# Another order of the seven products of the down projection, T3 summed into B22 in place, and a fixed order for the last rows

## Chip, cores and metric

The kernel runs on one core of a Trainium2 chip. The metric is the device time of one execution in microseconds (us); all times below are in us unless marked ns. The engines are TensorE (PE in the profile; PEld is its weight load), VectorE (DVE), ScalarE (ACT), GpSimd (POOL) and SyncE (SP), which here only issues transfers.

## What is computed

One decoder layer on 512 rows of 1024 channels in float32: two attention mixers and their projections, then a gated MLP with a short convolution, then a last normalisation. Only the end is touched by the change:

```python
def _conv_ffn(h, w_up, conv_w, conv_b, w_down):
    ...
    return (jax.nn.gelu(a, approximate=False) * g) @ w_down
...
        x = x + gate2 * _conv_ffn(h2, w_up[l], conv_w[l], conv_b[l], w_down[l])
    return _rmsnorm(x, final_g)
```

The down projection multiplies 512 x 2816 activations by 2816 x 1024 weights. `_rmsnorm` divides each row by the root of its mean square and multiplies by the gain `final_g`.

## The kernel before

**Seven products.** The down projection (lines 1489 to 1697) is a Strassen-Winograd product. The inner dimension is split in 11 pairs (`NPR`) of two blocks of 128 (a = 0, 1), the activations in two halves of 256 rows, the weights in two halves of 512 columns. B11, B12, B21, B22 are the blocks `wblock(g, a, hf)`. Seven products replace eight. Each is a pass over six groups of pairs (`grp`: five of two pairs, the last of one); each pass has 11 x 2 x 3 = 66 matmuls of 512 columns, because every operand is split in a high and a low part and three products of parts are taken (`split`, lines 113 to 115: ScalarE casts the high part, VectorE subtracts it to get the low part).

The passes (lines 1537 to 1545) and the bank pair each writes:

- m1 into dX, with B11; then B12 is summed onto the weights;
- m5 into dZ, with B11 + B12; then B22 is summed on;
- m6 into dY, with B11 + B12 + B22; then B21 is summed on;
- m7 into dW, with T3 = B12 + B22;
- p3 with B22, added to m5 in dZ;
- p2 with B21, added to m1 in dX;
- p4 with the sum of all four blocks, added to m7 in dW.

**The sums of weights.** The first three and the last use `chain`, five and a half buffers of 512 KB that stay. Each sum is an accumulating transfer in GpSimd's queue (line 1655), issued once VectorE has read the old content. T3, B22 and B21 are `streamed` (lines 1510 to 1518): a plain load by SyncE into one of four rotating buffers (`raw_tile`), and for T3 a second, accumulating transfer in GpSimd's queue. Two of the T3 groups have buffers of their own (`spare`).

**The results.** After m1, m6, m7, p3 and p2 the function `after_pass` makes a list of VectorE steps (with squares on ScalarE), and the main loop (lines 1674 to 1697) puts them between the preparations of the next pass as `EACH` says. So `e2 -= dW` (line 1589) follows m7, `e -= dZ` (line 1599) follows p3, and dX is read (line 1611) after p2. `x1` holds the residual in four tiles of 128 rows, t = 0 to 3, and two halves, hf = 0, 1; `res(t, hf)` is such a piece. Row tiles 0 and 1 are finished after p2: `square` takes the sum of squares, `stat_start` and `stat_end` (with `rstd_start`, `rstd_end`, lines 167 to 184) the inverse root, whose power runs on GpSimd, and line 1622 scales by root and gain on VectorE. Row tiles 2 and 3 are finished by `last_tile`, one after the other.

**What sets the order.** Within this stage a scheduler orders the instructions of each engine as they are recorded; an engine then takes its queue strictly in order. Three buffers each hold the high and low weight parts (`WB = 3`), so a cast for group g waits until TensorE has used group g - 3. In the last pass groups 3 to 5 are held back (`HOLD = 3`) and multiplied first for tile 2, then for tile 3.

## Time and profile before

| | us |
|---|---|
| three runs | 722.17, 719.83, 722.52 (median 722.17) |
| the profiled execution | 720.56 |
| its span (first to last event on the core) | 718.7 |
| granted TensorE clock, mean of the span | 0.994 of full speed |
| down projection, first matmul | 601.79 after the span's start |
| last matmul | starts at 708.59 |

The prediction reads three kinds of lines. A row of the timeline has start, duration, engine, line, operation and operands, then how often it is repeated; brackets give idle time of the engine just before and what ended it. A row of busy time by stage has the stretch and its length, then busy time and number of instructions for PE, PEld, DVE, ACT and POOL, the granted clock, the share of the transfer engines and GB/s. A row of a group has line, engine, operation, operands, count, busy time, mean ns of one, and idle time before. Buffer numbers are left out of the names, so `dc` is any bank of dX, dZ, dY, dW, and `chain_kvA` to `chain_outl` are the four buffers of the chain. Names such as `p4wh`, `p4wl`, `p4a` are the high and low weight parts and the activations of pass p4.

### The profile page before, as it was taken

The page shows a single profiled execution, that of the slowest core. Times are in us where ns is not written, and L with a number is a line of the kernel's source. Part 1 is how long each engine was busy: PE and PEld are TensorE (multiplying, and loading weights), DVE is VectorE, ACT ScalarE, POOL GpSimd, SP SyncE. Part 2 cuts the span into 40 slices and gives each one's busy share as a digit, 9 for nine tenths or more (in the row PEclk, how much of TensorE's full clock was granted, in tenths as well). Part 3 has the DMA queues.
Part 4 walks back from the last instruction along what each step waited for, and adds up shares of the span by engine and source line. Part 5 has one row for each costly group of instructions (what it writes and reads, how often), then busy time and mean ns, then how long its engine had stood idle before and what let it go on. Part 6 is the DMA issues. An engine that isn't in the chain of part 4 may idle for free. (4 is left out here: it accounts for less than half of the span.)

```text
span 718.7 us, 11251 instructions
## 1 busy us (share of the span) xinstructions
PE 691.1 (96%) x4172; PEld 603.1 (84%) x4172; DVE 589.8 (82%) x1121; ACT 381.9 (53%) x672; POOL 84.9 (12%) x101
## 2 busy tenths in 40 slices
PE   6998899999999999999999999999999999999994
PEld 6776688777777888888888999999999999778883
DVE  6998877887986674865479899888888999889996
ACT  4643756355553333432358756555656666556662
POOL 4000000000100110000012111111101212640000
PEclk9999999999999999999999999999999999999998
DMA  9986122543543665736717698876879769998502
GB/s 313 305 242 205 60 60 67 169 136 106 169 139 126 206 190 162 235 101 210 246 59 148 162 190 204 207 183 200 201 197 223 161 175 256 206 207 221 178 0 118
DMA packets 117367, 124.70 MB, mean 174 GB/s; under 512 B 4511, under 2 KB 93376, under 8 KB 117312
## 3 DMA queue, kind: packets, MB, share of 16 engines
q1 hardware_dynamic: 98254, 97.71, 43.0%
q0 software_dynamic: 18720, 25.73, 21.0%
q8 instruction: 33, 0.54, 0.3%
q10 hardware_dynamic: 338, 0.54, 0.2%
q14 instruction: 22, 0.18, 0.1%
HBM read 121.85 MB, written 2.11 MB: 172 GB/s over the span
## 5 line engine op out<-in xcount | busy, mean ns | idle before, releaser
L1112 PE MATMUL up<-t,m_whi 128*128 128x256 f32 x528 | 96.1, 283 | 0.0
L1112 PEld LDWEIGHTS up<-t,m_whi 128*128 128x128 f32 x528 | 82.4, 192 | 0.0
L1112 PE MATMUL up<-t,m_wlo 128*128 128x256 f32 x264 | 74.7, 283 | 0.1
L1112 PE MATMUL up<-bh,p_wlo 128*128 128x256 f32 x232 | 65.6, 283 | 0.3 <-DVE p_wlo L1055 0.3
L1112 PE MATMUL up<-bh,p_whi 128*128 128x256 f32 x232 | 65.6, 283 | 0.0
L1112 PE MATMUL up<-bl,p_whi 128*128 128x256 f32 x232 | 65.6, 283 | 0.0
L1112 PEld LDWEIGHTS up<-t,m_wlo 128*128 128x128 f32 x264 | 50.6, 192 | 0.3 <-DVE m_wlo L1055 0.3
L748 DVE SCALAR_TENSOR_TENSOR arow<-ra,cs,arow 128x512 f32<-128x512 f32 x56 | 41.9, 748 | 4.3 <-DMA ra<-in_w_ada_dram 3.6
L1112 PEld LDWEIGHTS up<-bh,p_wlo 128*128 128x128 f32 x232 | 44.5, 192 | 0.5 <-DVE p_wlo L1055 0.5
L1112 PEld LDWEIGHTS up<-bh,p_whi 128*128 128x128 f32 x232 | 44.5, 192 | 0.0
L1112 PEld LDWEIGHTS up<-bl,p_whi 128*128 128x128 f32 x232 | 44.5, 192 | 0.0
L1023 POOL DMA_DIRECT2D s<-in_w_up_dram x21 | 27.3, 1379 | 142.5 <-DMA s<-in_w_up_dram 54.3
L1055 DVE TENSOR_TENSOR m_wlo<-s,m_whi 128x1024 fp32r<-128x1024 f32 x31 | 37.7, 1217 | 2.0 <-ACT m_whi L1051 2.0
L1051 ACT CAST m_whi<-s 128x1024 fp32r<-128x1024 f32 x31 | 32.5, 1047 | 8.5 <-PE up L1112 4.6
L174 POOL TENSOR_TENSOR r<-ms,mhalf 128x1 f32<-128x1 f32 (+1 forms) x16 | 13.6, 848 | 172.4 <-DVE ms L172 105.7
L1112 PE MATMUL up<-t,p_whi 128*128 128x256 f32 x176 | 32.2, 283 | 0.0
L678 ACT ACTIVATE sd<-sd,dmx 128x128 f32<-128x128 f32 (+3 forms) x32 | 17.8, 557 | 22.2 <-DVE dmx L676 15.7
L761 POOL DMA_DIRECT2D mod_rows<-arow x8 | 4.3, 541 | 203.5 <-ACT arow L760 203.4
L1112 PEld LDWEIGHTS up<-t,p_whi 128*128 128x128 f32 x176 | 27.5, 192 | 0.0
L1119 ACT ACTIVATE gT<-a,cv 128x512 f32<-128x512 f32 x22 | 17.7, 814 | 17.6 <-DVE a L1154 17.3
L1051 ACT CAST p_whi<-wa 128x1024 fp32r<-128x1024 f32 x18 | 18.8, 1043 | 12.0 <-PE up L1112 7.2
L1112 PE MATMUL up<-t,p_wlo 128*128 128x256 f32 x88 | 24.9, 283 | 0.0
(476 smaller groups left out, 2120.8 us busy)
## 6 DMA issues: line engine op xcount, KB each, us to landing
ra<-in_w_ada_dram SPq DMA_DIRECT2D x32, 512.0 KB, 4.2
wa<-in_w_up_dram SPq DMA_DIRECT2D x22, 512.0 KB, 4.2
s<-in_w_up_dram SPq DMA_DIRECT2D x21, 512.0 KB, 4.8
s<-in_w_up_dram POOLq DMA_DIRECT2D x21, 512.0 KB, 6.7
adaw<-in_w_ada_dram SPq DMA_DIRECT2D x16, 512.0 KB, 5.0
w<-in_w_in_dram SPq DMA_DIRECT2D x12, 512.0 KB, 4.8
a<-in_w_up_dram SPq DMA_DIRECT2D x11, 512.0 KB, 4.7
b<-in_w_down_dram SPq DMA_DIRECT2D x10, 512.0 KB, 3.6
```

Source lines behind the costliest of these rows:

```text
L174: nc.gpsimd.tensor_tensor(r0, ms, mhalf[:, :n], ALU.pow)
L678: nc.scalar.activation(pm[m], pm[m], AF.Exp, bias=mx[:, m : m + 1], scale=slope, accum_out=lsum[:, m : m + 1])
L748: nc.vector.scalar_tensor_tensor(ac, r[:, a], cc, ac, ALU.mult, ALU.add)
L761: nc.gpsimd.dma_start(mod_rows[idx : idx + 1, hf * S : (hf + 1) * S], row)
L1023: nc.gpsimd.dma_start(dst, upblock(*blk), accum_op=ALU.add)
L1051: nc.scalar.copy(W[J, name][0], R[J, SRC[name]])
L1055: nc.vector.tensor_sub(lo, R[J, SRC[name]], hi.bitcast(F32))
L1112: nc.tensor.matmul(o[u], w[:, k, cu], b[:, k], start=name in ("p1", "m5", "p2") and k == 0 and x == 0, stop=k == 3 and x == 2, skip_group_ ...
L1119: nc.scalar.activation(grow(j), av[J][:, u], AF.Identity, bias=cv[:, 66 + j : 67 + j], scale=cv[:, 44 + j : 45 + j])
```

## The change

The passes run in the order m1, m5, m6, p2, p3, m7, p4. T3 has no buffers and loads of its own: B22 is loaded once, and when p3 has split a group, B12 is summed onto it in place by GpSimd's queue, for m7. Two groups of B22 have buffers of their own. The lists of steps move with their passes (`e2 -= dW` is now among the steps of the last pass), and the list after p2 is spread thinner (`EACH`).

The gain is multiplied in on GpSimd for row tiles 0 and 1 (four pieces) and for the second half of row tiles 2 and 3. Row tiles 0 and 1 are finished after p3, and ScalarE scales them by the root, one copy of 128 x 1024 each.

The last rows are written out in a fixed order on VectorE, ScalarE, TensorE and GpSimd (`last_rows`): tile 2 whole, tile 3 in two halves of 256 columns, for which the held back matmuls of tile 3 are split in two.

```diff
-    spare = {4: big.tile([P, 2, S], F32, tag="hhB", name="t3_4"), 5: big.tile([P, 1, S], F32, tag="hlB", name="t3_5")}
+    second = {g: big.tile([P, 2, S], F32, tag=t, name=f"b22_{g}") for g, t in enumerate(("hhB", "hlB"))}
...
+    def streamed(g):
+        r = raw_tile([P, grp[g][1] - grp[g][0], S], f"b21_{g}")
+        nc.sync.dma_start(r, wblock(g, 1, 0))
+        return r
+
+    def seconds(g):
+        if g not in second:
+            second[g] = raw_tile([P, grp[g][1] - grp[g][0], S], f"b22_{g}")
+        nc.sync.dma_start(second[g], wblock(g, 1, 1))
+        return second[g]
+
+    def thirds(g):
+        return second[g]
...
-        ("m7", dW, streamed("t3", ((0, 1), (1, 1))), lambda g: ablock(g, 0, 1), None, None),
-        ("p3", dZ, streamed("b22", ((1, 1),)), lambda g: s4[:, slice(*grp[g])], None, None),
-        ("p2", dX, streamed("b21", ((1, 0),)), lambda g: ablock(g, 1, 0), None, None),
+        ("p2", dX, streamed, lambda g: ablock(g, 1, 0), None, None),
+        ("p3", dZ, seconds, lambda g: s4[:, slice(*grp[g])], (0, 1), None),
+        ("m7", dW, thirds, lambda g: ablock(g, 0, 1), None, None),
...
+                    nc.gpsimd.tensor_mul(e2[:, u], res(2 + u, 1), fgb[:, S:])
...
+                    stat_start(u)
+                    nc.gpsimd.tensor_mul(res(u, 1), res(u, 1), fgb[:, S:])
...
-                yield lambda u=u: V.tensor_mul(e2[:, u], res(2 + u, 1), fgb[:, S:])
+                def scale(u=u):
+                    nc.scalar.activation(x1[:, u], x1[:, u], AF.Copy, scale=stat_end(u))
+                    nc.sync.dma_start(od[u * P : (u + 1) * P, :], x1[:, u])
+                yield scale
...
-                    stat_start(u)
+                    nc.gpsimd.tensor_mul(res(u, 0), res(u, 0), fgb[:, :S])
...
-            for u in two:
-                def scale(u=u):
-                    rs = stat_end(u)
-                    for hf in two:
-                        V.scalar_tensor_tensor(
-                            res(u, hf), res(u, hf), rs, fgb[:, hf * S : (hf + 1) * S], ALU.mult, ALU.mult
-                        )
-                    nc.sync.dma_start(od[u * P : (u + 1) * P, :], x1[:, u])
-                yield scale
...
+    def last_rows(todo):
+        man = ExitStack()
+        man.enter_context(
+            tc.manual_schedule(engines={nc.vector.engine, nc.scalar.engine, nc.tensor.engine, nc.gpsimd.engine})
+        )
+        c0, c1 = slice(0, H), slice(H, S)
+        part = [partial(parts[2 + u, 1]) for u in range(2)]
+        for g in todo:
+            multiply(len(passes) - 1, g, 0)
+        for sl in (c0, c1):
+            for g in todo:
+                multiply(len(passes) - 1, g, 1, sl)
+        for t in tasks:
+            t()
+        last_mul(0)
+        s0 = last_add(0)
+        last_gain(0)
+        last_mul(1, c0)
+        r0 = rstd_start(s0, 1, D, bp, plus=part[0])
+        s1 = last_add(1, c0)
+        last_gain(1, c0)
+        rs0 = bp.tile([P, 1], F32, tag="rs2", bufs=4, name="rse0")
+        rstd_end(rs0, *r0, 1, bp)
+        partial(s1, part[1])
+        last_mul(1, c1)
+        s2 = last_add(1, c1)
+        r1 = rstd_start(s2, 1, D, bp, plus=s1)
+        last_gain(1, c1)
+        last_scale(0, rs0)
+        last_scale2(0, rs0, nc.sync)
+        rs1 = bp.tile([P, 1], F32, tag="rs2", bufs=4, name="rse1")
+        rstd_end(rs1, *r1, 1, bp)
+        last_scale(1, rs1)
+        last_scale2(1, rs1, nc.scalar)
+        man.close()
...
-            nc.gpsimd.dma_start(chain[g], wblock(g, *add), accum_op=ALU.add)
+            nc.gpsimd.dma_start(w, wblock(g, *add), accum_op=ALU.add)
...
-    EACH = {3: (0, 2, 2, 2, 1, 1), 4: (0, 0, 2, 2, 1, 1), 5: (0, 0, 2, 2, 2, 2), 6: (0, 0, 2, 2, 1, 1)}
+    EACH = {3: (0, 2, 2, 2, 1, 1), 4: (0, 0, 1, 1, 1, 1), 5: (0, 0, 2, 2, 2, 2), 6: (0, 0, 2, 2, 1, 1)}
```

`last_mul`, `last_add`, `last_gain`, `last_scale` and `last_scale2` are the steps of `last_tile`, each for one tile or one range of its columns: product with the gate out of the bank, sum with the residual and square, product with the gain, scaling of the first half on VectorE, scaling of the second on ScalarE.

More of the change, by code (lines that the diff above doesn't have):

```diff
@@ L1508, in ablock @@
         return gT4[g][:, :, a, hf * H : (hf + 1) * H]
-    def streamed(name, blocks):
-        def get(g):
-            n = grp[g][1] - grp[g][0]
-            r = spare[g] if name == "t3" and g in spare else raw_tile([P, n, S], f"{name}_{g}")
-            nc.sync.dma_start(r, wblock(g, *blocks[0]))
-            for b in blocks[1:]:
-                nc.gpsimd.dma_start(r, wblock(g, *b), accum_op=ALU.add)
-            return r
-        return get
+    def streamed(g):
[9 more added lines that the diff above has]
+        return second[g]
     for g in range(len(grp)):
@@ L1628, in last_tile, with last_mul @@
-    def last_tile(u):
-        t = 2 + u
-        v = m1[:, u]
-        nc.vector.tensor_mul(v, dW[u], gate(0))
-        nc.vector.tensor_add(res(t, 0), res(t, 0), v)
-        square(t, 0)
-        nc.vector.tensor_mul(v, res(t, 0), fgb[:, :S])
-        stat_start(t)
-        rs = stat_end(t)
-        nc.vector.tensor_scalar_mul(res(t, 0), v, rs)
-        (nc.sync, nc.scalar)[u].dma_start(od[t * P : (t + 1) * P, :S], res(t, 0))
-        nc.scalar.activation(res(t, 1), e2[:, u], AF.Copy, scale=rs)
-        (nc.scalar, nc.sync)[u].dma_start(od[t * P : (t + 1) * P, S:], res(t, 1))
+    def last_mul(u, sl=slice(0, S)):
+        nc.vector.tensor_mul(m1[:, u, sl], dW[u][:, sl], gate(0)[:, sl])
@@ new lines, in last_add, with last_gain @@
+    def last_add(u, sl=slice(0, S)):
+        nc.vector.tensor_add(res(2 + u, 0)[:, sl], res(2 + u, 0)[:, sl], m1[:, u, sl])
+        sq = big.tile([P, S], F32, tag="sq2", name=f"sqe{u}_{sl.start}")
+        s1 = bp.tile([P, 1], F32, tag="ss2", bufs=8, name=f"sse{u}_{sl.start}")
+        nc.scalar.activation(sq[:, sl], res(2 + u, 0)[:, sl], AF.Square, accum_out=s1)
+        return s1
+    def last_gain(u, sl=slice(0, S)):
+        nc.vector.tensor_mul(m1[:, u, sl], res(2 + u, 0)[:, sl], fgb[:, sl])
@@ new lines, in partial, with last_scale, last_scale2 @@
+    def partial(s1, plus=EPS):
+        nc.vector.tensor_scalar(s1, s1, 1.0 / D, plus, ALU.mult, ALU.add)
+        return s1
+    def last_scale(u, rs):
+        nc.vector.tensor_scalar_mul(res(2 + u, 0), m1[:, u], rs)
+        nc.sync.dma_start(od[(2 + u) * P : (3 + u) * P, :S], res(2 + u, 0))
+    def last_scale2(u, rs, q):
+        nc.scalar.activation(res(2 + u, 1), e2[:, u], AF.Copy, scale=rs)
+        q.dma_start(od[(2 + u) * P : (3 + u) * P, S:], res(2 + u, 1))
+    def last_rows(todo):
[33 more added lines that the diff above has]
+        man.close()
@@ L1658, in prepare, with multiply @@
         ops[i, g] = ah, al, wh, wl
-    def multiply(i, g, u):
+    def multiply(i, g, u, sl=slice(0, S)):
         name, bank2 = passes[i][:2]
@@ L1669, in multiply @@
                 nc.tensor.matmul(
-                    bank2[u], a[:, q, cu], b[:, q], start=first_mm and x == 0, stop=last_mm and x == 2,
+                    bank2[u][:, sl], a[:, q, cu], b[:, q, sl], start=first_mm and x == 0, stop=last_mm and x == 2,
                     skip_group_check=name not in first,
@@ L1682 @@
                 next(tasks)()
-        assert next(tasks, None) is None
         tail = HOLD if i == len(passes) - 1 else 0
@@ L1688 @@
         if tail:
-            for u in range(2):
-                for g in range(NG - tail, NG):
-                    multiply(i, g, u)
-                last_tile(u)
+            last_rows(range(NG - tail, NG))
         else:
```

## The prediction

> **What bounds the kernel now.** I read the page's busy shares first, then busy time by stage, then TensorE's rows for its gaps, then the rows of the other queues around each gap.

> ```profile
> span 718.7 us, 11251 instructions
> PE 691.1 (96%) x4172; PEld 603.1 (84%) x4172; DVE 589.8 (82%) x1121; ACT 381.9 (53%) x672; POOL 84.9 (12%) x101
> ...
> 480.00:520.00 40.00, 40.00 (x336) 40.00 (x335) 34.74 (x50) 22.98 (x35) 4.83 (x6) 1.00 0.81 201
> 601.60:633.60 32.00, 30.84 (x136) 24.82 (x135) 28.79 (x43) 19.00 (x27) 16.33 (x14) 1.00 1.06 207
> 633.60:693.50 59.90, 59.66 (x263) 49.42 (x264) 54.47 (x75) 37.10 (x56) 6.92 (x6) 1.00 0.65 165
> 693.50:709.00 15.50, 15.47 (x68) 12.17 (x66) 14.66 (x29) 7.07 (x13) 1.51 (x3) 1.00 0.17 69
> 709.00:718.70 9.70, 0.00 (x0) 0.00 (x0) 4.03 (x11) 2.17 (x4) 1.06 (x2) 0.76 0.28 108
> ```

> TensorE (first pair of each stage row) is busy nearly everywhere, and only the down projection (601.6 onwards) is touched. Its seven passes of 66 matmuls run at full clock; VectorE (third pair) has 54.5 us of work in 59.9, so it is never far ahead. A change gains where TensorE waits now or after its last matmul, and loses where it makes TensorE wait. These are the rows where it waits, starts the last pass, and ends:

> ```profile
> 622.90 0.50 PE L1669 MATMUL dc<-m5wl,m5a 128*128 128x512 f32 x1 [0.27 <-DVE m5wl L115]
> ...
> 632.33 0.39 PE L1669 MATMUL dc<-m6wh,m6a 128*128 128x512 f32 x1
> 633.84 0.50 PE L1669 MATMUL dc<-m6wl,m6a 128*128 128x512 f32 x1 [1.13 <-DVE m6wl L115]
> ...
> 693.59 0.39 PE L1669 MATMUL dc<-p4wh,p4a 128*128 128x512 f32 x1
> ...
> 704.82 0.50 PE L1669 MATMUL dc<-p4wl,p4a 128*128 128x512 f32 x1
> ...
> 708.59 0.39 PE L1669 MATMUL dc<-p4wh,p4a 128*128 128x512 f32 x1
> 710.39 0.68 DVE L1631 TENSOR_TENSOR pairs<-dc,g2b 128x512 f32<-128x512 f32 x1
> 714.12 0.72 ACT L1639 ACTIVATE x<-chain_outl,rsd 128x512 f32<-128x512 f32 x1 [1.56 <-DVE rsd L184]
> 714.87 0.33 SPq L1640 DMA_DIRECT2D out_dram<-x  x1
> ```

> From 633.84 to 693.59 are 263 matmuls, 0.227 each, so a pass is 15.0. The last matmul ends at 708.98 (708.59 + 0.39), the last arithmetic at 714.84, 5.86 later; the last store fills the rest of the span.

> **The change, part by part.** I keep the clock of before: p2 and m7 trade the fourth and sixth of seven slots, p3 stays fifth, p4 last.

> *T1, sums taken out of the crowded start.* GpSimd's queue sums T3 early now; the change sums b12 into b22 during p3.

> ```profile
> 610.86 1.20 POOL L1516 DMA_DIRECT2D t<-in_w_down_dram  x1 [5.44 <-DMA t<-in_w_down_dram]
> 611.68 1.62 POOL L1655 DMA_DIRECT2D chain_kvB<-in_w_down_dram  x1
> ...
> 620.54 1.05 ACT L114 CAST m5wh<-chain_kvB 128x1024 fp32r<-128x1024 f32 x1 [2.88 <-DMA chain_kvB<-in_w_down_dram]
> ...
> 621.62 1.23 DVE L115 TENSOR_TENSOR m5wl<-chain_kvB,m5wh 128x1024 fp32r<-128x1024 f32 x1 [3.06 <-ACT m5wh L114]
> ```

> One T3 sum holds the queue for 5.44 until its first half has landed. Behind it stand the chain sums; kvB's arrives so late that ScalarE idles 2.88 and VectorE 3.06, and VectorE, hardly idle from there to m6, delivers m5wl and m6wl late. Without that wait kvB is issued some 4 earlier, and one 512 KB sum fewer runs beside it. Both stalls should go. Price: 632.33 to 633.84 is 1.51 where 0.23 is normal (1.28); the m5 gap is 0.27 plus the 0.16 by which a 0.39 matmul normally overlaps its successor; each restart takes 0.50 rather than 0.39 (0.22 for both). Sum -1.9, from 0 (all stays) to -1.9.

> *T2, p4 behind m7 in the same banks.* This decides. Now p4 adds to dW long after L1589 has read m7's result from it. Afterwards p4 follows m7 directly, so its first matmul must wait until that subtraction (`e2 -= dW`) has read the bank. In the built program's order VectorE reaches that subtraction only after the low halves of p4's groups 0, 1 and 2.

> ```profile
> 663.18 0.69 DVE L1589 TENSOR_TENSOR chain_outl<-chain_outl,dc 128x512 f32<-128x512 f32 x1 [0.44 <-PE dc L1669]
> ...
> 688.44 1.29 DVE L115 TENSOR_TENSOR p4a<-gT,p4a 128x512 fp32r<-128x512 f32 x2
> 688.61 0.19 ACT L1552 ACTIVATION_READ_ACCUMULATOR sqd<-x 128x1 f32 x1
> 689.70 1.06 ACT L114 CAST p4wh<-chain_kvA 128x1024 fp32r<-128x1024 f32 x1 [0.91 <-PE dc L1669]
> ...
> 690.79 1.23 DVE L115 TENSOR_TENSOR p4wl<-chain_kvA,p4wh 128x1024 fp32r<-128x1024 f32 x1 [1.06 <-ACT p4wh L114]
> ...
> 693.90 1.05 ACT L114 CAST p4wh<-chain_kvB 128x1024 fp32r<-128x1024 f32 x1
> ...
> 695.45 1.22 DVE L115 TENSOR_TENSOR p4wl<-chain_kvB,p4wh 128x1024 fp32r<-128x1024 f32 x1
> ```

> Floor: the cast for group 2 takes the buffer of the previous pass's last group, so it cannot start before that pass's last matmul ends, at 693.75 (one 0.227 before 693.59, plus 0.39; the row has 693.90). Cast 1.05, low half 1.22, subtraction 0.69, handoffs 0.1: p4 starts at 696.8 at best, +3.2. Had the subtraction stood first (as L1589 did at 663.18) it would cost some 0.3.

> ScalarE makes it later. Row tiles 0 and 1 are now scaled by ScalarE (two 128x1024 copies), and in its queue both stand ahead of p4's first cast. The second copy needs the inverse root of row tile 1, which needs GpSimd's power, which stands in GpSimd's queue behind a product by the gain of the same tile, which needs the second square (accumulator read until 688.80). With d for one GpSimd product: 688.80 + 0.1 + d, power 0.6, two small VectorE steps 0.45, copy 1.0 gives p4's first cast at 690.95 + d. From there to the end of the subtraction: cast and handoff 1.1, three low halves 1.14 apart, one p4a 0.6 (two took 1.29), subtraction and handoff 0.74, in all 5.85.

> ```profile
> L150 POOL TENSOR_SCALAR_AFFINE_SELECT ddf<-ddf 128x512 f32<-128x512 f32 x1 | 0.6, 608 | 0.0
> L435 POOL MEMSET va<- 128x2048 f32 x1 | 1.8, 1804 | 0.0
> ...
> 367.90 0.68 DVE L1253 TENSOR_TENSOR early<-wa,early 128x512 fp32r<-128x512 f32 x1
> 368.07 0.93 POOL L174 TENSOR_TENSOR r<-ms,mhalf 128x1 f32<-128x1 f32 x1 [3.68 <-DVE ms L172]
> ...
> 373.37 0.69 DVE L1232 TENSOR_TENSOR bl<-braw,bh 128x512 fp32r<-128x512 f32 x1
> 373.53 0.93 POOL L174 TENSOR_TENSOR r<-ms,mhalf 128x1 f32<-128x1 f32 x1 [4.53 <-DVE ms L172]
> 377.01 0.55 POOL L174 TENSOR_TENSOR r<-ms,mhalf 128x1 f32<-128x1 f32 x1 [2.54 <-DVE ms L172]
> ```

> No GpSimd product of 128x512 is in the trace. One of one input took 0.61; I take d = 1.2 for two inputs, with ends 0.6 and 1.8 (the longest GpSimd arithmetic row). That gives a first cast at 692.15 and p4 at 698.0, +4.4 (+3.8 to +5.0).

> The last rows say more. The power took 0.93 twice when a VectorE sum or difference of two SBUF tiles was running, and both times it ended 0.4 after that one (368.58, 374.06); without one it took 0.55. So GpSimd waited. Whether a long GpSimd product holds VectorE likewise no row shows; I take it that it does, since the exclusion is there in one direction. VectorE here runs little but such differences. Then the two products of the slot cost VectorE, ahead of the second root, about 1.2 each, less what its gaps hide: +2.2, from +1.4 (GpSimd gets in behind the running difference) to +3.2 (it waits for a gap). T2 = +6.6; bounds +3.2 and +8.2. [...]

> *T3, VectorE relieved.* These instructions leave VectorE:

> ```profile
> L1622 DVE SCALAR_TENSOR_TENSOR x<-x,rsd,fgbr 128x512 f32<-128x512 f32 x4 | 2.8, 746 | 0.0
> L1608 DVE TENSOR_TENSOR chain_outl<-x,fgbr 128x512 f32<-128x512 f32 x2 | 1.3, 688 | 0.0
> ```

> That is 4 x 0.746 + 2 x 0.688 = 4.4. But TensorE felt VectorE's load after m6 only at 704.82, a restart of 0.50 that lost some 0.2: -0.2. Elsewhere the matmuls themselves hid these instructions, so the rest of the relief is worth nothing.

> *T4, the last tile in two column halves.* 336 matmuls of mostly 256 columns took 40.00, 0.119 each; 30 of them against 15 of 0.227 is +0.2.

> *T5, after the last matmul.* Now VectorE reaches the last tile 1.41 after 708.98, held by the tile before. Afterwards that tile's three steps run under the last 3.6 of matmuls. But the first half's VectorE product has, in the built program, its wait on the very last matmul, so the halves don't overlap: one half's three steps come ahead of the other's chain. A half step I estimate at 0.4, between half of 0.68 and all of it. The chain of a whole tile is 4.45 now (710.39 to 714.84); three half steps ahead add 1.2, the shorter product, sum and square take 0.8 off, the other tile's small statistics in between add 0.35: 5.2 against 5.86, -0.6 (0 to -1.4). The stores are as now.

> Sum: -1.9 + 6.6 - 0.2 + 0.2 - 0.6 = +4.1.

> The profiled execution took 720.56 (1.9 outside its span); the median shown is 722.17 (719.83 to 722.52). The mean of the four is 721.3, and on it I put the sum: 725.4.

> **The rivals.**

> *No mutual hold.* GpSimd products run beside VectorE: T2 = +4.4 and the sum is +1.9, 723.2, not measurably slower. For it: no row shows VectorE held. Against: the two rows of 0.93. The point is whether the second root is ready by about 691.

> *The in-place sum comes late.*

> ```profile
> 660.92 1.22 DVE L115 TENSOR_TENSOR p3wl<-b,p3wh 128x1024 fp32r<-128x1024 f32 x1
> ...
> 674.74 1.06 ACT L114 CAST p2wh<-b 128x1024 fp32r<-128x1024 f32 x1 [0.91 <-PE dc L1669]
> ...
> chain_kvA<-in_w_down_dram POOLq DMA_DIRECT2D x6, 512.0 KB, 10.2
> t<-in_w_down_dram POOLq DMA_DIRECT2D x5, 512.0 KB, 7.1
> ```

> b12 may be added only when p3's split has read b22 (slot five, 662.14), and m7's cast wants it 12.6 later. Sums took 7 to 10 in the crowded stretch; here they run almost alone. From 12.6 on each microsecond goes to the split. At 13, with the last two sums also behind a GpSimd product, I estimate +2: 727.4.

> *Not slower.* VectorE takes the subtraction from dW as soon as m7 ends, as L1589 did at 663.18: T2 is +0.3 instead of +6.6, and with T5 at its end the sum is -1.9 + 0.3 - 0.2 + 0.2 - 1.4 = -3.0, 718.3. It decides if the bank is free before p4's first low half is needed. The order of the built program speaks against it; it is also the price if my reading of that wait is wrong.

> **How the numbers follow.** Forecast 0.58, no hold 0.28, late sum 0.10, not slower 0.04. The forecast's own range is 723.5 to 728 (T2 from +5.8 to +8.2, T1 from -1.9 to -1). About 0.5% (3.6) is what a measurement of this kernel can tell from no change; the forecast lies on both sides of that: 0.42 of its 0.58 above, the late sum all above, no hold all within, the last rival half within and half beyond on the fast side. So faster 0.02, same 0.46, slower 0.52. The range 722.0 to 728.8 reaches from no hold with T5 near its end to the late sum with a T2 of 8, and leaves out the last rival and the far ends.

> **What would show it.** T1: no gap at m5 and m6, kvB's sum near 607. T2: one TensorE gap of 3 to 8 ahead of p4's first matmul, ended by the subtraction from dW, with ScalarE's two row copies ahead of p4's first cast. The hold: GpSimd products of 128x512 and VectorE rows that start when these end; without it the gap is near 4.4. T5: 5.2 from the last matmul to the last copy. The prediction is wrong if there is no gap before p4, or if gaps appear inside m7 (late sums).

## The result and the profile after

Medians of four runs each: 728.50 (727.06 to 729.48) after, 721.32 (719.83 to 722.52) before. The ratio is 1.0094, 95% interval 1.0077 to 1.0111: about 6.8 us slower. The forecast was 725.4. The profiled execution took 728.95, its span is 727.2.

The first row is the page's busy shares of the changed kernel; compare PE with 691.1 before:

```profile
PE 693.7 (95%) x4187; PEld 605.9 (83%) x4187; DVE 590.6 (81%) x1119; ACT 383.1 (53%) x676; POOL 95.0 (13%) x107
```

TensorE is busy 2.6 us longer for the same work, so part of that work ran slower. Busy time by stage, the six passes up to m7, then the gap in two pieces, then p4 in two pieces (the granted clock is the number after the last "x" group):

```profile
603.40:693.20 89.80, 89.80 (x398) 74.10 (x396) 82.86 (x117) 54.14 (x80) 35.74 (x29) 1.00 0.85 166
693.20:697.50 4.30, 0.17 (x1) 0.00 (x0) 2.06 (x4) 4.00 (x6) 0.00 (x0) 1.00 0.59 244
697.50:700.60 3.10, 0.00 (x0) 0.00 (x0) 3.10 (x5) 1.74 (x3) 0.00 (x0) 0.50 0.00 0
700.60:704.30 3.70, 3.64 (x9) 2.90 (x10) 3.70 (x7) 0.09 (x1) 0.10 (x1) 0.50 0.00 0
704.30:717.80 13.50, 13.50 (x74) 11.57 (x72) 6.60 (x10) 5.01 (x10) 2.83 (x2) 1.00 0.01 2
```

The first six passes run without a break. Then TensorE stands still, and from 697.5 to 704.3 its clock is at half. TensorE's own rows at the places shown before, and around p4's start:

```profile
603.40 0.40 PE L1719 MATMUL dc<-m1wh,m1a 128*128 128x512 f32 x1
...
633.37 0.39 PE L1719 MATMUL dc<-m6wh,m6a 128*128 128x512 f32 x1
633.60 0.39 PE L1719 MATMUL dc<-m6wl,m6a 128*128 128x512 f32 x1
...
692.99 0.39 PE L1719 MATMUL dc<-m7wh,m7a 128*128 128x512 f32 x1
700.66 0.77 PE L1719 MATMUL dc<-p4wh,p4a 128*128 128x512 f32 x1 [7.28 <-DVE chain_outl L1594]
701.22 0.63 PE L1719 MATMUL dc<-p4wl,p4a 128*128 128x512 f32 x1
701.65 1.05 PE L1719 MATMUL dc<-p4wh,p4a 128*128 128x512 f32 x2
...
717.52 0.28 PE L1719 MATMUL dc<-p4wh,p4a 128*128 128x256 f32 x1
```

At m6 the second matmul follows after 0.23, where 1.51 passed before. p4 would have started at 693.22 and starts at 700.66: **a gap of 7.44**, ended by the subtraction from dW. The next matmuls start 0.43 apart instead of 0.227. The p4 pass takes 17.14 (700.66 to 717.80), before 15.39. The three other queues ahead of p4, each from the timeline. GpSimd's, from kvB's first sum on:

```profile
609.48 1.20 POOL L1705 DMA_DIRECT2D chain_kvB<-in_w_down_dram  x1 [2.44 <-DVE m1wl L115]
...
686.69 1.46 POOL L1613 TENSOR_TENSOR x<-x,fgbr 128x512 f32<-128x512 f32 x1 [10.15 <-ACT sqd L1557]
688.31 1.82 POOL L174 TENSOR_TENSOR r<-ms,mhalf 128x1 f32<-128x1 f32 x1 [0.16 <-DVE ms L172]
690.10 1.28 POOL L1613 TENSOR_TENSOR x<-x,fgbr 128x512 f32<-128x512 f32 x1
692.23 0.93 POOL L174 TENSOR_TENSOR r<-ms,mhalf 128x1 f32<-128x1 f32 x1 [0.84 <-DVE rsd L184]
```

VectorE's, with the first step after the last matmul as its last row:

```profile
686.90 1.26 DVE L172 SCALAR_TENSOR_TENSOR ms<-ssd,ssd 128x1 f32<-128x1 f32 x1
...
690.16 1.25 DVE L180 SCALAR_TENSOR_TENSOR rt<-r,ms 128x1 f32<-128x1 f32 x1 [0.46 <-POOL r L174]
691.33 0.68 DVE L115 TENSOR_TENSOR p4a<-gT,p4a 128x512 fp32r<-128x512 f32 x1
691.93 0.15 DVE L172 SCALAR_TENSOR_TENSOR ms<-ssd,ssd 128x1 f32<-128x1 f32 x1
...
693.45 0.16 DVE L184 SCALAR_TENSOR_TENSOR rsd<-rt,r 128x1 f32<-128x1 f32 x1
695.82 2.36 DVE L115 TENSOR_TENSOR p4wl<-chain_kvA,p4wh 128x1024 fp32r<-128x1024 f32 x2 [2.21 <-ACT p4wh L114]
698.09 0.69 DVE L115 TENSOR_TENSOR p4a<-gT,p4a 128x512 fp32r<-128x512 f32 x1
698.70 1.22 DVE L115 TENSOR_TENSOR p4wl<-chain_kvB,p4wh 128x1024 fp32r<-128x1024 f32 x1
699.83 1.28 DVE L1594 TENSOR_TENSOR chain_outl<-chain_outl,dc 128x512 f32<-128x512 f32 x2
...
717.84 0.42 DVE L1632 TENSOR_TENSOR pairs<-dc,g2b 128x256 f32<-128x256 f32 x1 [1.45 <-PE dc L1719]
```

ScalarE's, with the last arithmetic as its last row:

```profile
692.25 1.15 ACT L1617 ACTIVATE x<-x,rsd 128x1024 f32<-128x1024 f32 x1 [2.66 <-DVE rsd L184]
693.70 1.15 ACT L1617 ACTIVATE x<-x,rsd 128x1024 f32<-128x1024 f32 x1 [0.30 <-DVE rsd L184]
694.75 1.98 ACT L114 CAST p4wh<-chain_kvA 128x1024 fp32r<-128x1024 f32 x2
...
722.59 0.72 ACT L1653 ACTIVATE x<-chain_outl,rse 128x512 f32<-128x512 f32 x1 [0.89 <-DVE rse L184]
```

Read them as one chain: GpSimd's first product (686.69), VectorE's step `ms` beside it (686.90), the first power (688.31), VectorE's first root step (690.16), a split of p4's activations (691.33), the second `ms` (691.93), the second power (692.23), the second root (693.45), ScalarE's second copy (693.70), p4's first casts (694.75), three low halves, the subtraction (699.83), TensorE. The second product (690.10) is on the chain because the root step of 690.16 waits beside it: VectorE steps on a 128x1 column take 1.26 and 1.25, each ending when a GpSimd product ends; without one the same steps take 0.15 and 0.22. From the first matmul of m1 to the end of the last arithmetic (the **stage**) it is 119.91, before 113.05: +6.86, the whole loss.

The stage starts 1.6 later in this profile (603.40 against 601.79), for a reason far ahead of it, in code that the change leaves alone. Busy time of one stretch there:

```profile
60.00:80.00 20.00, 16.89 (x85) 12.33 (x86) 15.05 (x50) 8.63 (x27) 0.00 (x0) 0.83 0.50 161
```

It is the stretch from 60 to 80 of the changed kernel, at a granted clock of 0.83; in the kernel before it is 1.00. Over the profiles of this study the stage starts between 599.9 and 603.4. So kernels are compared below by the stage where a term is wanted, and by the ratio, against the kernel before on the same chip, for the whole.

### The profile page after: what moved, and what is told of

It reads as the page before. It is cut to its first block, busy times and chain, and to the rows that moved or that the text cites. A ratio compares the mean times of both kernels' runs of the same rounds, so it can differ in the third digit from the quotient of the medians.

```text
span 727.2 us, 11282 instructions
## 1 busy us (share of the span) xinstructions
PE 693.7 (95%) x4187; PEld 605.9 (83%) x4187; DVE 590.6 (81%) x1119; ACT 383.1 (53%) x676; POOL 95.0 (13%) x107
## 2 busy tenths in 40 slices
DMA packets 115864, 121.83 MB, mean 168 GB/s; under 512 B 4415, under 2 KB 93280, under 8 KB 115808
## 5 line engine op out<-in xcount | busy, mean ns | idle before, releaser
L174 POOL TENSOR_TENSOR r<-ms,mhalf 128x1 f32<-128x1 f32 (+1 forms) x16 | 14.5, 904 | 120.0 <-DVE ms L170 54.7
L678 ACT ACTIVATE sd<-sd,dmx 128x128 f32<-128x128 f32 (+3 forms) x32 | 17.8, 557 | 22.2 <-DVE dmx L676 15.4
## 6 DMA issues: line engine op xcount, KB each, us to landing
ra<-in_w_ada_dram SPq DMA_DIRECT2D x32, 512.0 KB, 4.2
wa<-in_w_up_dram SPq DMA_DIRECT2D x22, 512.0 KB, 4.1
s<-in_w_up_dram SPq DMA_DIRECT2D x21, 512.0 KB, 4.9
s<-in_w_up_dram POOLq DMA_DIRECT2D x21, 512.0 KB, 6.4
adaw<-in_w_ada_dram SPq DMA_DIRECT2D x16, 512.0 KB, 4.8
w<-in_w_in_dram SPq DMA_DIRECT2D x12, 512.0 KB, 4.4
a<-in_w_up_dram SPq DMA_DIRECT2D x11, 512.0 KB, 4.6
b<-in_w_down_dram SPq DMA_DIRECT2D x10, 512.0 KB, 4.0
```

The lines of the kernel that those rows point to most:

```text
L174: nc.gpsimd.tensor_tensor(r0, ms, mhalf[:, :n], ALU.pow)
L678: nc.scalar.activation(pm[m], pm[m], AF.Exp, bias=mx[:, m : m + 1], scale=slope, accum_out=lsum[:, m : m + 1])
```

## Experiments

All start from the changed kernel unless said. "Pass" is p4's, from its first matmul to the end of the last, "tail" from there to the end of the last arithmetic.

| kernel | ratio (95%) | gap | pass | tail | stage |
|---|---|---|---|---|---|
| before | 1 | 0 | 15.39 | 5.86 | 113.05 |
| after | 1.0094 (1.0077 to 1.0111) | 7.44 | 17.14 | 5.51 | 119.91 |
| e1 gains on VectorE | 0.9971 (0.9958 to 0.9983) | 0.35 | 15.43 | 5.46 | 111.03 |
| e2 subtraction earlier | 1.0047 (1.0034 to 1.0060) | 5.69 | 17.43 | 5.52 | 118.44 |
| e3 copies later | 1.0006 (0.9994 to 1.0018) | 2.34 | 17.02 | 5.52 | 114.67 |
| e4 roots and copies behind p4 | 0.9960 (0.9948 to 0.9972) | 0.35 | 15.98 | 5.63 | 111.79 |
| e5 TensorE busy, 100 matmuls | 1.0132 (1.0102 to 1.0161) | filled | 15.41 | 5.51 | 121.83 |
| e6 early sums again | 1.0033 (1.0012 to 1.0053) | 0.35 | 15.96 | 5.64 | 117.40 |
| e7 e1 + GpSimd products | 1.0021 (1.0005 to 1.0038) | 2.72 | 15.43 | 5.46 | 114.51 |
| e8 e1 + GpSimd memsets | 0.9963 (0.9935 to 0.9990) | 0.35 | 15.44 | 5.46 | 111.04 |
| e9 e1, last tile whole | 0.9952 (0.9935 to 0.9969) | 0.35 | 15.24 | 4.86 | 110.25 |
| e10 TensorE busy, 64 matmuls | 1.0061 (1.0040 to 1.0081) | filled | 15.42 | 5.52 | 118.16 |
| e12 memsets for products | 1.0055 (1.0034 to 1.0076) | 4.97 | 18.00 | 5.52 | 118.30 |

Gap, pass, tail and stage are those of one profiled execution; the ratio is over all runs. In e2 and e6 the two differ by some 2 us (stage +5.4 and +4.4 against before, ratio worth +3.4 and +2.4; e6's twelve runs lie between 718.06 and 728.40). Why isn't shown.

**The chain ahead of p4 (e1 to e4).**

```diff
-                    nc.gpsimd.tensor_mul(res(u, 1), res(u, 1), fgb[:, S:])
+                    nc.vector.tensor_mul(res(u, 1), res(u, 1), fgb[:, S:])
```

(e1; so for all three such lines.)

> The changed kernel with its six 128x512 products by the gain on VectorE instead of GpSimd; all else as changed (in the built order VectorE then also takes the subtraction from dW one low half earlier). Theory A (the wait ahead of p4 is made by the chain GpSimd product, power, second root, ScalarE's row copies, p4's casts): the power comes early, the gap ahead of p4 falls from 7.4 to 0.3-0.6, TensorE's clock stays at 1.00 after it, the p4 pass takes 15.4-15.6 instead of 17.1, and the time is about 719.5 (728.5 - 7.1 - 1.75). Theory B (the floor of the prediction: p4's third cast must wait for m7's last matmul and the subtraction stands behind it): gap 3.2 or more, 723 to 724.

TensorE's row of e1:

```profile
693.57 0.47 PE L1719 MATMUL dc<-p4wh,p4a 128*128 128x512 f32 x1 [0.19 <-DVE chain_outl L1594]
```

The wait for the subtraction is still there and costs 0.35. 719.27, faster than before: theory A. In its built order VectorE takes the subtraction behind p4's first low half, so theory B's floor no longer applies; e1 alone doesn't tell how much is GpSimd and how much this place.

```diff
-    EACH = {..., 6: (0, 0, 2, 2, 1, 1)}
+    EACH = {..., 6: (0, 2, 0, 2, 1, 1)}
```

> The changed kernel with the two subtractions from dW one group earlier in VectorE's queue (behind p4's second low half instead of its third); GpSimd's products and ScalarE's copies as changed. Theory A (the chain behind GpSimd makes p4's casts late): the gap only loses one low half and one p4a, 7.4 to about 5.7, the clock still falls to half afterwards, about 726.5. Rival (only the place of the subtraction in VectorE's queue decides): gap 0.3, about 719.5.

Gap 5.69, as theory A has it: with the chain as it is, the place of the subtraction is worth one low half and one p4a, not the whole gap. The stage is 1.5 shorter than the changed kernel's. The time, 724.22, is 2.3 below the expected 726.5, more than the stage explains.

```diff
+            if i == 6 and g == 4:
+                for t in later:
+                    t()
...
+            if i == 5:
+                later = list(tasks)
...
-5: (0, 0, 2, 2, 2, 2)
+5: (0, 0, 2, 2, 2, 0)
```

> The changed kernel with ScalarE's two 128x1024 row copies asked for after p4's fifth group instead of ahead of p4's first cast; the two small root steps stay in VectorE's queue ahead of p4's first low half, GpSimd's products stay. Theory A: what is left is the second root behind GpSimd, then one low half and the subtraction: gap 3.2 to 3.7. If TensorE's clock falls only after long gaps, the p4 pass is back at 15.4-15.6 and the time is about 722.8 (728.5 - 4.0 - 1.75); if it falls after any gap of some us, 724.5. Rival (the copies on ScalarE are not in the way): gap near 7, 728.

721.20. The gap is 2.34, shorter than expected, since the scheduler also moved the subtraction, behind the first low half, and put the copies behind p4's first cast only. By its rows what still delays that low half is the second root. The pass takes 17.02 all the same: of the two cases named, the one in which the clock falls after any gap of some us came.

e4 writes the order of the last pass out by hand, with e3's edit at g == 5:

```diff
+        if i == 6:
+            man = ExitStack()
+            man.enter_context(tc.manual_schedule(engines={nc.vector.engine, nc.scalar.engine}))
...
-6: (0, 0, 2, 2, 1, 1)
+6: (2, 0, 0, 2, 1, 1)
```

> The changed kernel with GpSimd's products kept, but in the last pass VectorE and ScalarE take a written order: the subtraction from dW right behind p4's first low half, the two roots and the two row copies behind p4's last split. Theory A: gap ahead of p4 0.3-0.5, clock 1.00, some 0.6 of small waits at p4's last group, about 720. Rival (the products on GpSimd hold VectorE so much that p4's splits are late wherever roots and copies stand): gap 2 or more, 723 or more.

718.46 with GpSimd's products in place. So the products don't make p4 late by themselves; what stands behind them in the queues of p4's first group does.

**How much is the mutual hold (e7, e8, e12).** The hold is that a VectorE step and a GpSimd product keep each other waiting. e7 adds to e1 `nc.gpsimd.tensor_mul(junk, al, fgb[:, :S])` after each of m7's first five groups (`al`: the group's low activations, `junk`: memory with no later reader); e8 puts a 128x1 product and three `nc.gpsimd.memset(junk, 0.0)` in its place.

> The kernel with the gains on VectorE (719.3), plus five GpSimd products of 128x512 with two SBUF inputs in the m7 slot, into memory that nothing reads any more. Hold theory: a VectorE operation with two SBUF inputs waits while a GpSimd product runs and the other way round; VectorE rows of 0.69 and 1.22 that overlap a product grow by up to its 1.3, about 4 to 6 us in all, TensorE waits ahead of p4 by 1 to 4 us: 720 to 725. Rival (only GpSimd waits): VectorE rows keep their lengths, the products grow, 719.3.

> The same kernel with the gains on VectorE, plus in the place of each of the five products a product of 128x1 and three memsets of 128x512 on GpSimd (about the same GpSimd time, no SBUF input). Hold theory in the form that it is the reading of SBUF that excludes: VectorE rows keep 0.69 and 1.22, no wait of TensorE, 719.3. Rival (any GpSimd work slows VectorE): rows as long as with the products, 720 to 725.

VectorE's low halves of m7 in e7:

```profile
677.02 2.00 DVE L115 TENSOR_TENSOR m7wl<-b,m7wh 128x1024 fp32r<-128x1024 f32 x1
...
679.54 1.21 DVE L115 TENSOR_TENSOR m7wl<-b,m7wh 128x1024 fp32r<-128x1024 f32 x1
...
681.88 2.32 DVE L115 TENSOR_TENSOR m7wl<-b,m7wh 128x1024 fp32r<-128x1024 f32 x1
```

GpSimd's products beside two of them, in e7 too:

```profile
676.64 1.29 POOL L1734 TENSOR_TENSOR s<-m7a,fgbr 128x512 f32<-128x512 f32 x1 [0.69 <-DVE m7a L115]
681.50 1.61 POOL L1734 TENSOR_TENSOR s<-m7a,fgbr 128x512 f32<-128x512 f32 x1 [3.57 <-DVE m7a L115]
```

and low halves of m7 in e8 with memsets beside them:

```profile
676.89 1.22 DVE L115 TENSOR_TENSOR m7wl<-b,m7wh 128x1024 fp32r<-128x1024 f32 x1
...
679.23 1.22 DVE L115 TENSOR_TENSOR m7wl<-b,m7wh 128x1024 fp32r<-128x1024 f32 x1
```

which are these rows of GpSimd in e8:

```profile
676.49 1.69 POOL L1736 MEMSET s<- 128x512 f32 x3
...
679.43 1.70 POOL L1736 MEMSET s<- 128x512 f32 x3
```

A low half that issues while a product runs ends 1.1 later (2.32 against 1.22); beside memsets none is longer. GpSimd waits as well: the product of 681.50 takes 1.61 because VectorE's row ahead (681.28, 0.68 long) ends at 681.96. So the exclusion goes both ways, and beside memsets, whose rows have no input, there is none. The times are 723.42 and 717.92.

In e12 the changed kernel keeps its queues as they are, and each of the six products becomes a 128x1 product and two memsets:

```diff
-                    nc.gpsimd.tensor_mul(res(u, 1), res(u, 1), fgb[:, S:])
+                    nc.gpsimd.tensor_mul(dead[:, :1], res(u, 1)[:, :1], fgb[:, S:S + 1])
+                    for _ in range(2):
+                        nc.gpsimd.memset(dead, 0.0)
```

> The changed kernel with every one of GpSimd's six products of 128x512 replaced by a product of 128x1 and two memsets of 128x512 into memory that nothing reads any more: the same place in GpSimd's queue and about the same GpSimd time (0.3 and 2 x 0.56 against 1.3), the order on VectorE and ScalarE unchanged, but next to no reading of SBUF (these six products by the gain are left out of the computation, which moves nothing else). Forecast's theory (of the gap of 7.4, some 2.2 come from the mutual hold, the rest from the chain of queues): gap ahead of p4 4.8 to 5.5, time 2 below the changed kernel, about 726.5 (ratio 1.0065). Rival without a hold: gap 7.2 to 7.6, ratio 1.0095.

Gap 4.97 with GpSimd at least as busy as before (2.17 and 1.29 in the place of the two products of 1.46 and 1.28), 7.44 with the products: the hold's share of the gap is 2.47, the queues' 4.97. The time is 724.79, below the expected 726.5, although the pass is longer than in any other kernel (18.00).

**The slow start of p4 (e5, e10, e11).** 100 (e5) or 64 (e10) matmuls of a constant go between m7 and p4:

```diff
+            for x in range(64):
+                nc.tensor.matmul(dX[0][:, :P], onesr, onesr, start=x == 0, stop=x == 63)
```

> The changed kernel with 100 extra 128x128 matmuls of a constant (into a bank that nothing reads any more; no result depends on them) between m7's last matmul and p4's first, so that TensorE isn't idle in the gap; p4 still waits for the subtraction from dW. Clock theory: p4 still starts 7.4 late, but the clock stays at 1.00 and the p4 pass takes 15.3-15.6 instead of 17.14: about 726.7. Rival (p4's first 3.6 us are slow for another reason: operands, VectorE, the half-width matmuls): p4 pass 17.1, 728.5 or more. If the extra matmuls last longer than the gap, p4 starts later by that much.

> The changed kernel with 64 instead of 100 extra matmuls of a constant in the gap ahead of p4. 100 of them took 11.0 us, so 64 take 7.0 and end before the subtraction from dW: p4 starts 7.4 late as in the changed kernel, the clock stays at 1.00, the p4 pass takes 15.4 instead of 17.1, so the time is 1.7 below the changed kernel's 728.5, about 726.8. If the slow start had another cause: 728.5.

e10, gap and start of p4 (compare 0.50 in the rows of the changed kernel):

```profile
690.00:697.40 7.40, 7.24 (x65) 7.12 (x64) 5.15 (x8) 5.69 (x8) 0.00 (x0) 1.00 0.35 144
697.40:701.00 3.60, 3.59 (x16) 2.99 (x17) 3.60 (x7) 0.03 (x1) 0.04 (x1) 1.00 0.00 0
```

p4 waits as long as ever, the clock stays at 1.00 and the pass takes 15.42: the clock made it 17.14. The 100 matmuls lasted longer than the gap (p4 3.65 later still, 730.30). With 64 the useless work makes the kernel faster: ratio 1.0061 against 1.0094, stage 118.16 against 119.91. The time, 724.51, is lower than the expected 726.8, as with e2.

> The same kernel as the run with ScalarE's copies later, looked at a second time. If the length of a gap alone decides whether the clock falls, its gap of 2.3 ahead of p4 again makes the p4 pass 17.0. If it also matters how the gap lies in some fixed beat of the throttle (the gap of 2.7 in the run with extra products left the clock at 1.00), the pass may take 15.4 this time with the same gap.

Again 2.34 and 17.04, in a single run. The loss repeats. But the fall lay in nearly the same place: at 694.5 in e3, and in e11 at 694.6, an estimate from its rows (two matmuls from 694.38 take 0.86, where two take 0.62 at full clock and 1.05 at half). So e11 doesn't test the second theory; e7 does. e3 by time, the gap and the half clock:

```profile
691.50:694.50 3.00, 0.82 (x4) 0.56 (x4) 2.83 (x4) 3.00 (x4) 0.00 (x0) 1.00 0.38 157
694.50:697.90 3.40, 3.40 (x10) 2.62 (x9) 3.38 (x4) 1.98 (x3) 0.00 (x0) 0.50 0.42 170
```

and e7, where a longer gap left it at 1.00:

```profile
692.30:695.00 2.70, 0.15 (x1) 0.02 (x1) 2.70 (x6) 2.70 (x4) 0.00 (x0) 1.00 0.41 168
695.00:698.40 3.40, 3.39 (x15) 2.81 (x16) 3.40 (x5) 2.89 (x6) 0.00 (x0) 1.00 0.43 175
```

**T1 undone (e6).** e4 with two of the old sums back in the queue, at g = 0 and 2 of m1:

```diff
+            if i == 0 and g in (0, 2):
+                nc.sync.dma_start(second[g // 2], wblock(g, 1, 1))
+                nc.gpsimd.dma_start(second[g // 2], wblock(g, 0, 1), accum_op=ALU.add)
```

> The kernel of the run with roots and copies behind p4 (718.5), with two sums of 512 KB put back into GpSimd's queue at the start of the down projection, one ahead of the chain sums and one ahead of kvB's, each with its own load, as T3's two sums stood in the kernel before (their result is overwritten later). T1's theory (a sum that waits for its load holds the queue and makes the chain sums late): TensorE waits at m5 and m6 again, 1.0 to 1.9 in all, 719.5 to 720.4. Rival (what fell with the change were the bytes of five sums, not the place of two in the queue): no wait, 718.5.

GpSimd's queue in e6, the second added sum and kvB's first:

```profile
613.50 1.20 POOL L1735 DMA_DIRECT2D b<-in_w_down_dram  x1 [8.82 <-DMA b<-in_w_down_dram]
614.22 1.71 POOL L1705 DMA_DIRECT2D chain_kvB<-in_w_down_dram  x1
```

and TensorE's waits ahead of p4 in e6, all but the one for the subtraction:

```profile
622.84 0.49 PE L1719 MATMUL dc<-m5wh,m5a 128*128 128x512 f32 x1 [1.21 <-ACT m5wh L114]
624.10 0.80 PE L1719 MATMUL dc<-m5wl,m5a 128*128 128x512 f32 x1 [0.76 <-DVE m5wl L115]
...
636.69 0.50 PE L1719 MATMUL dc<-m6wl,m6a 128*128 128x512 f32 x1 [1.22 <-DVE m6wl L115]
```

The stalls are back at m5 and m6, behind a sum that waits for its load and a kvB sum issued 13.2 after m1's start (6.1 in the changed kernel). The mechanism is shown; the size was missed, +5.6 on the stage of e4 instead of 1.0 to 1.9, because this load lands later than T3's did (the queue is held 8.82, not 5.44) and the m5 stalls also halve the clock for a while (0.50 granted from 623.9 to 627.3).

**The halves (e9).** e1 with tile 3 in one piece, matmuls and steps:

```diff
-        for sl in (c0, c1):
-            for g in todo:
-                multiply(len(passes) - 1, g, 1, sl)
+        for g in todo:
+            multiply(len(passes) - 1, g, 1)
```

> The kernel with the gains on VectorE (0.9971 of the kernel before, 719.3), with the last row tile in one piece of 512 columns instead of two halves, in matmuls and in the steps behind them. T5's theory (the first half's product waits for the very last matmul, so the halves only add steps): from the end of the last matmul to the end of the last arithmetic 4.5 to 4.7 instead of 5.46, and the p4 pass 0.2 shorter (15 matmuls of 0.227 instead of 30 of 0.119): 1.0 to 1.2 less, ratio 0.9955. Rival (the halves do shorten the chain, as half of the columns is done earlier): 5.5 to 6, ratio 0.9975 or more.

Tail 4.86 instead of 5.46, pass 15.24 instead of 15.43. The tail is 0.2 longer than expected, the direction is T5's: the halves cost 0.8 in all. 716.81, ratio 0.9952: e9 beats the kernel before and the changed one.

## Why the prediction held, and what it missed

The direction was right and the cause was the one named, but the loss was 6.9 on the stage and not 4.1. That 728.50 lies inside the stated range is partly luck: it lies beyond the forecast's own 723.5 to 728, and 0.3 below the upper end of 728.8, which was put there for late sums, and these didn't come. Its steps:

| step | forecast | measured | from |
|---|---|---|---|
| T1 sums out of the start | -1.9 | -1.98 | m1's start to p4's earliest start, 89.82 against 91.80 |
| T2 p4 behind m7 | +6.6 | +7.44 | the gap |
| T3 VectorE relieved, T4 halves' matmuls, and the clock | 0.0 | +1.75 | pass 17.14 against 15.39 |
| T5 tail | -0.6 | -0.35 | 5.51 against 5.86 |
| sum | +4.1 | +6.86 | stage |

**T1** was right to 0.1, and e6 shows the mechanism; kvB's sum was issued at 609.48, 6.1 after m1's start, against 9.9 before.

**T2** was right in its links but one. The power was to stand behind the product in GpSimd's queue. In e12, without the hold, it does (memsets end and power starts at 688.2). In the changed kernel the product ends at 691.38 and the power starts at 692.23, since VectorE's `ms` ahead of it stands behind the held root step and a split. From p4's first cast to p4 it forecast 5.85; the rows give 700.66 - 694.75 = 5.91. Mis-sized is what lies ahead of that cast. Without a hold it forecast 4.4, e12 gives 4.97: GpSimd's work for one product is nearer 1.3 than 1.2, the power takes 0.71 rather than 0.6, and a copy 1.15 rather than 1.0. The hold was put at 2.2, from two powers of 0.93; it is 2.47. The floor, the cast of the third group, was no floor of the change but of one queue order: e1 and e4 place the subtraction ahead of that group and wait 0.35.

**The step that failed** stands in one sentence at the head of the working: "I keep the clock of before". A gap of 6.6 was forecast, and nothing asked what TensorE does after standing still so long. It cost 1.72 in the pass, 15.42 in e10 against 17.14 in the changed kernel. The trace of before has no gap over 1.3 between matmuls of this stage. But the prediction's own last stage row gives a clock of 0.76 for the 9.7 after the last matmul: the clock fell to half 5.1 after TensorE had stopped (at 714.04), so a gap of 6.6 could be expected to reach that. What such a fall costs stands in no row that the prediction reads; the runs show it: p4 ran at half clock for 3.65 (700.66 to 704.31), for a pass 1.72 longer. With that term the sum would have given 727.1.

**T4** holds: 15.43 - 15.24 = 0.19 between e1 and e9. **T3**: no wait at p4's last group, but as p4 starts 7.4 late VectorE has the time anyway; that the relief did it isn't shown. **T5** was right that the first half waits for the very last matmul (717.84, idle 1.45, ended by TensorE); the rest of the chain is 0.3 longer than estimated.

**The rivals.** *No mutual hold* falls with e7, e8 and e12. *The in-place sum comes late* falls with the first row of the stages: no break inside m7. *Not slower* was the right mechanism for another kernel: the point it names, the bank read before p4's low halves need VectorE, is met in e1 and e4, which gain 2.0 and 1.3 on the stage.

## What to carry to other kernels

When two accumulating products in the same bank become neighbours, look at what stands in the reader's queue ahead of the read that frees the bank, and follow it through every engine: here the read took 0.7 and its queue made it 7.4 late. Before moving work to an idle engine, ask what its result is queued in front of, and whether its operands exclude a busier engine (a low half of 1.22 took 2.32 in e7). A forecast gap on TensorE can have a second price, the half clock after it (1.6 to 2.6 in e2, e3, e12 and the changed kernel, nothing in e7): add it to the sum, or fill the gap.
